# A product of the second step moved ahead of product 5 of the first, sums prepared in the head alone, and two transposes one product later

## The chip, the cores and the metric

The kernel runs on one core of one Trainium2 chip. The metric is the device time in microseconds. Three runs of the kernel before took 1656.38, 1656.97 and 1657.07 us, a median of 1656.97. The engines are named as the profile names them: PE is TensorE, DVE is VectorE, ACT is ScalarE, POOL is GpSimd and SP is SyncE. POOL and SP issue DMAs here.

## The reference

The program is a small decoder trunk on 512 tokens of 1024 features in float32, two layers deep. Each layer has a feed-forward network, a token mixer and a second feed-forward network, each with a residual and a layer norm behind it. The mixer is block-sparse attention in the first layer and multi-scale pooling in the second.

```
def swiglu(x, w_gu, w_down):
    g, u = jnp.split(x @ w_gu, 2, axis=-1)
    return (jax.nn.silu(g) * u) @ w_down

x = layer_norm(ALPHA * x + 0.5 * swiglu(x, ffn_w_gu[i, 0], ffn_w_down[i, 0]), ...)
x = layer_norm(ALPHA * x + mixer(x), ...)
x = layer_norm(ALPHA * x + 0.5 * swiglu(x, ffn_w_gu[i, 1], ffn_w_down[i, 1]), ...)
```

The inner width of the feed-forward network is 2816. The change touches neither what is computed nor the number of multiplications; it moves work.

## The kernel before, in words

**Stages.** The kernel numbers its six blocks: n=0, n=2, n=3 and n=5 are feed-forward networks (ffn), n=1 is attention and n=4 is pooling. In the profiled execution the ffn n=2 begins at about 550 us, n=3 at about 875 us, n=5 at about 1310 us. The first ffn takes another form (the flag `eight`), and the change leaves it alone.

**Products.** A float32 product is made of three matmuls: a weight tile is split into `hi` and `lo`, and lines 110, 111 and 112 add lo times x, hi times x's low part and hi times x's high part. A block of the first matrix product is not computed as eight sub-products but, in Strassen's way, as seven, numbered 1 to 7, with sums of weight blocks and sums of x blocks as operands. A step `jj` is a group of 512 inner features; the pair (i, jj) is product i of step jj. Each product has 24 matmuls of 128x512 in two halves (q = 0 and 1, each with the weights of one *unit*). `order()` at line 180 writes the order of all products by hand, since PE's queue is scheduled manually. Before the change an ffn begins (1,1), (2,1), (1,2), (5,1), (6,1), (7,1), (3,1), (4,1), (2,2), (6,2) and so on.

**Weights.** A step has two *quads*, one for each half of the contraction. A quad loads its four blocks a11, a12, a21, a22 as pieces: p11, p12, p22, and the two sums s1 = a21 + a22 and s3 = a21 + a11, which are made by a load on SP's queue (L302) and a DMA with accumulation on POOL's queue (L304). Product 6 needs p11 + s1. In steps 1 and 2 each quad makes it on VectorE in place by itself (`apart`, L158), once the accumulating DMA has landed. `prepare()` turns a unit into `hi` and `lo`: ScalarE copies hi (L105) and VectorE subtracts (L106). For the products in `BY_TRANSFER` ScalarE writes both (L336, L337) and a POOL DMA subtracts (L338). `run_ahead()` prepares as many units ahead as there is room. Only PE's order is written by hand: the recording layer schedules the instructions of the other engines and sets the order of their queues. `tc.issue_after` keeps instructions behind a named one.

**The head of an ffn.** The four token tiles t of the block before end in a layer norm: residual add (L519 in attention and pooling, L984 in an ffn), statistics (L523, L529), a square root on ScalarE, a reciprocal (L535), and the scaling of `ax` (L545). Eight PE transposes of 128x128 for each tile (L487, called T(0) to T(3) here) turn it to feature-major, and ScalarE and VectorE copy and split the result into the `x` operands. T(0) and T(1) lie in the last product of the block before. `late` holds the calls for T(2) and T(3); `head()` pops one of them after each half of (1,1). The products 1, 6 and 5 are copied out of PSUM by ScalarE (`keep`, L736); product 6 in step 1 in two halves.

**Gated rows.** A finished product pair is gated by ScalarE and VectorE (L727, L728) and then turned by four PE transposes (L761) in `to_features`. With products 5 and 4 it takes what waits in the list `waiting`.

Of the kernel before, what the change touches and what calls it, by code (L numbers as in the profile page):

```python
# [56 lines left out]
PARTS = 5  # L57
# [26 lines left out]
def trunk(ctx, tc, x_in, xt, rel_bias, ln_g, ln_b, w_gu, w_gq, w_dq, w_dh, w_v, a_in, a_out, b_in, b_group, b_scale, b_out, onehot, out):  # L84
# [34 lines left out]
            self.size = math.prod(src.shape[1:]) / 1024  # L119
            pieces.append(self)  # L120

    pieces, units, loaded, behind = [], [], [], {}

    def plain(src, lean=False):
        p = Piece(src)
        units.append((lambda: p.tile, (p,), src if lean else None))
# [51 lines left out]


    def order(eight):  # L180
        o = [(1, 1), (2, 1)] + ([(6, 1), (5, 1)] if eight else [(1, 2), (5, 1), (6, 1)])
        o += [(7, 1), (3, 1)] + [(1, 2)] * eight + [(4, 1)]
        steps = STEPS[not eight]
        for jj, following in zip(steps[1:], steps[2:] + (None,)):
            seven = [(i, jj) for i in (2, 6, 5, 7, 3, 4)]
            after = [(1, following)] if following is not None else []
            if jj == MIDDLE:
                group = [(i, FF) for i in LATER]
                o += seven[:-1] + group[:1] + seven[-1:] + group[1:] + after
            else:  # L190
                o += seven[:-1] + after + seven[-1:]
        return o + [(i, FF + 1) for i in DEEP]
# [24 lines left out]
            units.append((lambda: p.tile, (p,)))  # L217

    BY_TRANSFER = ((1, 1), (2, 1), (1, 2))

    def in_turn(quads, kinds):
        pieces[-5 * len(quads):] = [q.pieces[k] for k in kinds for q in quads]
# [18 lines left out]
    def ffn_units(l, m):  # L241
        eight = (l, m) == (0, 0)
        if eight:
            for i in FIRST:
                plain(w_gu[l, m, i])
        made = {}
        for i, jj in ORDERS[not eight]:
            lean = not eight and (i, jj) in BY_TRANSFER
            if (i, jj) == (1, 2) and not eight:
                for q in range(2):  # L250
                    plain(w_gq[l, m, 2 + q, 0], lean)
                b1 = pieces[-12:]
                pieces[-12:] = b1[0:2] + b1[4:6] + b1[2:4] + b1[10:] + b1[6:10]
                continue
            if jj not in made:
                if jj == 0:
                    made[jj] = [Quad(w_gu[l, m])]
                    pieces[-5:] = [made[jj][0].pieces[k] for k in (0, 2, 1, 3, 4)]
                elif jj == FF:
                    made[jj] = in_turn([Quad(w_dq[l, m, 0]), Quad(w_dq[l, m, 1]), narrow(Quad(w_dh[l, m]))], (0, 2, 1, 3, 4))  # L260
                elif jj == FF + 1:
                    made[jj] = in_turn([Deep(w_dq[l, m, q]) for q in (2, 3, 4)], range(5))
                else:
                    made[jj] = two_quads(w_gq[l, m], 2 * (jj - 1))
                for q in made[jj]:
                    if not eight and jj in (1, 2):
                        q.apart()
                    if i == 2:
                        q.p11.uses -= 1
            for q in made[jj]:  # L270
                q.unit(i, lean)

# [34 lines left out]
    def free():  # L307
        return SLOTS - RAW - 2 * PARTS - sum(held)
# [35 lines left out]

    def run_ahead(most=99):
        load_ahead()
        while len(parts) < min(len(units), taken[0] + most, retired[0] + PARTS + max(0, free() - 2) // 2 + early[0] + sum(i >= retired[0] for i in guests)):
            load_needed()
            prepare()
            load_ahead()  # L350
# [348 lines left out]
    def ffn(n, x, dest):  # L699
        with tc.tile_pool(name=f"ffn{n}", bufs=1) as fp:  # L700
# [47 lines left out]
                waiting.append((out, 4 * jj - 4 + 2 * half, h))  # L748
                return ins

            def to_features(i, kept_back=1):

                row = 0
                while i in (5, 4) and len(waiting) > (i == 4) * kept_back:
                    out, f, h = waiting.pop(0)
                    row += 1
                    turn[0] += row < 3
                    tp = banks(TURNED + turn[0] % 2 if row < 3 else sums_at[1], 1, f"ft{n}_{f}_{h}")[0].rearrange("p (c s) -> p c s", c=2)
                    for c in range(2):
                        for t in range(2):  # L760
                            nc.tensor.transpose(tp[:, c, t * P:(t + 1) * P], out[:, t, c * P:(c + 1) * P], ident)  # L761
                    nc.scalar.activation(features(f, 2)[:, :, h * 256:(h + 1) * 256], tp, AF.Copy)
# [177 lines left out]
            def products(i, jj, b, amid=lambda q: None, outer=3, count=2):  # L940

                if i in (1, 2, 5):
                    accs[jj, BANKS[i]] = bank_pair(((SECOND if i != 1 else sums_at[jj]) + 4 * eight) % 8)
                acc = accs[jj, BANKS[i]]

                def one(w, k0, ts, first, last):
                    wh, wl = w
                    ks = wh.shape[-1] // 512
                    for k in range(ks):
                        c = slice(k * 512, (k + 1) * 512)  # L950
                        for t in ts:
                            mm3(acc[:, t], *b(k0 + k, t), wh[:, c], wl[:, c], first and k == 0 and i in (1, 2, 5),
                                last and k == ks - 1 and i in (2, 3, 4), True)

                for q in range(min(outer, count)):
                    one(weights(), 2 * q, range(2), q == 0, q == count - 1)
                    amid(q)
                ws = [weights() for q in range(outer, count)]
                for t in range(2):
                    for q, w in enumerate(ws, outer):  # L960
                        one(w, 2 * q, (t,), q == 0, q == count - 1)
                        amid((q, t))
                return acc

            def head(i, jj):

                def amid(q):
                    if i == 1:
                        late.pop(0)()
                    if (i, q) == (1, 1):  # L970
                        while len(parts) < taken[0] + 2:
                            load_needed()
                            prepare()
                        with tc.issue_after(x.last.ins):
                            next(sums)
                return amid
# [32 lines left out]
            def down_second(i):  # L1009

                def amid(q):
                    if i == 4:
                        if q == (1, 0) and not last:
                            late.pop(0)()
                        if q != (2, 1) and q[1] == 1:
                            retire()
                    else:
                        if i == 2 and q == 2 and not last:
                            late.pop(0)()
                        if q < 2:  # L1020
                            retire()

                acc = products(i, FF + 1, operand(1, i), amid, 0 if i == 4 else 3, 3)
                half, d, sign = OUT[i]
                ts = range(2 - 2 * half, 4 - 2 * half)
                if i == 4:
                    for k, t in enumerate(ts):
                        add(t, d, acc[:, k], sign)
                        norms[t].stats(d)
                        normalized(t)  # L1030
                else:
                    add(slice(ts[0], ts[0] + 2), d, acc, sign)
                    if i in (3, 7, 2):
                        for t in ts:
                            if i != 7:
                                norms[t] = LayerNorm(n, t, 0.5)
                            norms[t].stats(d)
                    if i == 7:
                        if last:
                            params[:] = ln_params(n)  # L1040
                        for t in ts:
                            normalized(t)
                        early[0] = (2, 0, 4, 2, 0, 0)[n]
                if i == 1:
                    to_features(5)
                for _ in range({1: 2, 5: 1, 6: 1, 3: 2}.get(i, 0)):
                    next(operands[1])
                retire()

            for i, jj in ORDERS[not eight]:  # L1050
                if jj == FF:
                    down_first(i)
                    to_features(i)
                    continue
                if jj > FF:
                    down_second(i)
# [15 lines left out]
                    room(jj)  # L1072
                if jj == 0:
                    in_seven(i)
                    to_features(i)
                    retire()
                    continue
                if not eight and (i, jj) in ((1, 1), (2, 1)):
# [5 lines left out]
                if i in DONE:  # L1084
                    ins = finish(i, jj, acc)
                    if (i, jj) in RESIDUAL:
                        update_residual(ins)
                to_features(i, 2 if not eight and jj == 1 else 1)
                if not eight and (i, jj) in ((1, 1), (2, 1), (1, 2), (6, 1)):
                    if (i, jj) != (1, 1):  # L1090
                        with tc.issue_after(x.last.ins):
# [353 lines left out]
```

## Time and profile before

| what | value |
|---|---|
| median of the runs | 1656.97 us (1656.38 to 1657.07) |
| the profiled execution's own time | 1656.67 us |
| its span | 1654.9 us |
| PE busy | 1638.9 us, 99% |
| DVE busy | 1362.3 us, 82% |
| ACT busy | 953.0 us, 58% |
| POOL busy | 174.8 us, 11% |
| bytes moved by DMA | 315.62 MB, 191 GB/s over the span |

The span runs from the first to the last instruction in the trace; the time of an execution has some 1.8 us around it. In a row of the timeline stand the start in us, the duration, the engine, the line, the operation, what it writes and reads, the shape, and in square brackets how long the engine stood idle before it and what ended that. A matmul of 128x512 is shown with 0.39 us, but the next starts after 0.23 us: they are pipelined. In a row of the windows stand the stretch, its length, then for PE, weight loads, DVE, ACT and POOL the busy time and the number of instructions, and at the end the granted TensorE clock, the mean busy share of the DMA engines and GB/s. The line "DMA to landing" gives the least, the median and the greatest time from the issue of the DMAs of one line in one stretch to their landing.

### The profile page before, as it was taken

How to read it: one execution, taken by the hardware profiler on the slowest of the kernel's cores; microseconds unless marked ns; L12 is line 12 of the kernel's file. 1: busy time of each engine (PE TensorE's matmuls, PEld its weight loads, DVE VectorE, ACT ScalarE, POOL GpSimd, SP SyncE). 2: the span in 40 equal slices, each digit the busy share in tenths (PEclk: the TensorE clock that was granted, in tenths of full speed). 3: DMA queues.
4: the chain of work that ended last, by engine and by line, in shares of the span. 5: the costliest groups of instructions: out<-in, count | busy, mean ns of one | idle time of the engine just before them, and what ended most of it. 6: DMA issues, size and time to landing. Idle time of an engine off the chain costs nothing.

```text
span 1654.9 us, 21597 instructions
## 1 busy us (share of the span) xinstructions
PE 1638.9 (99%) x8051; PEld 1382.7 (84%) x8051; DVE 1362.3 (82%) x1719; ACT 953.0 (58%) x1279; POOL 174.8 (11%) x224
## 2 busy tenths in 40 slices
PE   9999999999999999999999999999999999999997
PEld 8888888898888888988888889888898878888886
DVE  7778898988575887878898878898987698779899
ACT  5556555666445665555567655556554665555562
POOL 1101101000011011101111111011000201110110
PEclk9999999999999999999999999999999999999999
DMA  9678688825157488757878887578734878866882
GB/s 300 187 224 247 151 218 227 243 71 178 52 135 197 114 242 218 201 141 212 239 214 208 251 229 186 144 214 228 225 108 125 195 201 223 245 148 176 229 205 77
DMA packets 99913, 315.62 MB, mean 191 GB/s; under 512 B 10144, under 2 KB 23496, under 8 KB 99808
## 3 DMA queue, kind: packets, MB, share of 16 engines
q1 hardware_dynamic: 71904, 214.99, 37.1%
q0 software_dynamic: 27904, 99.26, 32.7%
q8 instruction: 63, 1.03, 0.3%
q14 instruction: 42, 0.34, 0.1%
HBM read 312.09 MB, written 4.74 MB: 191 GB/s over the span
## 4 chain that ended last, share of the span: by engine, by line
PE 89%; DVE 6%; ACT 2%; issue 1%; DMA 1%; SPq 0%; DVEq 0%; ACTq 0%
PE banks L110 29%; PE banks L112 29%; PE banks L111 29%; PE banks L761 2%; DVE lo L106 2%; ACT st L495 1%; DVE x L106 1%; DVE st L429 1%; PE banks L487 1%; ACT x L105 1%; DVE st L523 1%; DVE ax L984 0%; PE banks L1194 0%; DMA raw<-in_ffn_w_gu 0%; DVE ax L542 0%
## 5 line engine op out<-in xcount | busy, mean ns | idle before, releaser
L105 ACT ACTIVATE hi<-raw 128x1024 fp32r<-128x1024 f32 (+1 forms) x478 | 500.3, 1057 | 334.2 <-DVE lo L106 121.2
L106 DVE TENSOR_TENSOR lo<-raw,hi 128x1024 fp32r<-128x1024 f32 (+1 forms) x478 | 576.8, 1218 | 130.1 <-ACT hi L105 88.3
L110 PE MATMUL banks<-lo,x 128*128 128x512 f32 x1144 | 449.3, 393 | 2.1 <-ACT kept L736 0.9
L112 PE MATMUL banks<-hi,x 128*128 128x512 f32 x1144 | 446.0, 390 | 0.0
L111 PE MATMUL banks<-hi,x 128*128 128x512 f32 x1144 | 445.4, 389 | 0.0
L110 PEld LDWEIGHTS banks<-lo,x 128*128 128x128 f32 x1144 | 214.8, 188 | 49.1 <-ACT kept L736 3.3
L112 PEld LDWEIGHTS banks<-hi,x 128*128 128x128 f32 x1144 | 214.8, 188 | 45.3
L111 PEld LDWEIGHTS banks<-hi,x 128*128 128x128 f32 x1144 | 215.0, 188 | 43.1
L110 PE MATMUL banks<-lo,h 128*128 128x512 f32 x436 | 171.4, 393 | 0.0
L112 PE MATMUL banks<-hi,h 128*128 128x512 f32 x436 | 169.8, 389 | 0.0
L111 PE MATMUL banks<-hi,h 128*128 128x512 f32 x436 | 169.7, 389 | 0.0
L110 PE MATMUL banks<-x,hi 128*128 128x256 f32 (+1 forms) x488 | 152.7, 313 | 0.5 <-ACT hi L105 0.5
L112 PE MATMUL banks<-x,lo 128*128 128x256 f32 (+1 forms) x488 | 152.0, 311 | 1.0 <-DVE lo L106 1.0
L111 PE MATMUL banks<-x,hi 128*128 128x256 f32 (+1 forms) x488 | 151.7, 311 | 0.0
L304 POOL DMA_DIRECT2D raw<-in_ffn_w_gq x80 | 71.0, 890 | 653.7 <-DMA raw<-in_ffn_w_gq 210.0
L152 DVE TENSOR_TENSOR raw<-raw,raw 128x1024 f32<-128x1024 f32 (+1 forms) x86 | 102.8, 1195 | 23.6 <-DMA raw<-in_ffn_w_gq 12.3
L110 PEld LDWEIGHTS banks<-x,hi 128*128 128x128 f32 x488 | 93.0, 191 | 6.6 <-ACT hi L105 0.9
L112 PEld LDWEIGHTS banks<-x,lo 128*128 128x128 f32 x488 | 93.0, 191 | 6.6 <-DVE lo L106 1.6
L111 PEld LDWEIGHTS banks<-x,hi 128*128 128x128 f32 x488 | 93.0, 191 | 5.3
L112 PEld LDWEIGHTS banks<-hi,h 128*128 128x128 f32 x436 | 81.8, 188 | 17.2
L111 PEld LDWEIGHTS banks<-hi,h 128*128 128x128 f32 x436 | 81.9, 188 | 16.5
L110 PEld LDWEIGHTS banks<-lo,h 128*128 128x128 f32 x436 | 81.9, 188 | 16.3
(229 smaller groups left out, 2246.0 us busy)
## 6 DMA issues: line engine op xcount, KB each, us to landing
raw<-in_ffn_w_gq SPq DMA_DIRECT2D x206, 512.0 KB, 5.0
raw<-in_ffn_w_dq SPq DMA_DIRECT2D x100, 512.0 KB, 4.8
raw<-in_ffn_w_gq POOLq DMA_DIRECT2D x80, 512.0 KB, 7.3
raw<-in_ffn_w_dq POOLq DMA_DIRECT2D x52, 512.0 KB, 7.7
ax<-in_ln_b POOLq DMA_DIRECT2D x20, 512.0 KB, 8.8
raw<-in_ffn_w_gu SPq DMA_DIRECT2D x18, 512.0 KB, 5.1
raw<-in_a_w_in SPq DMA_DIRECT2D x16, 512.0 KB, 3.8
raw<-in_ffn_w_dh SPq DMA_DIRECT2D x20, 256.0 KB, 2.8
```

What stands on the lines that cost most here:

```text
L105: nc.scalar.activation(hi, src, AF.Copy)
L106: return nc.vector.tensor_tensor(lo, src, hi.bitcast(F32), op=ALU.subtract)
L110: nc.tensor.matmul(acc, sh, ml, start=first, stop=False, skip_group_check=shared)
L111: nc.tensor.matmul(acc, sh, mh, start=False, stop=False, skip_group_check=shared)
L112: nc.tensor.matmul(acc, sl, mh, start=False, stop=last, skip_group_check=shared)
L152: nc.vector.tensor_tensor(d, d, more, op=ALU.add)
L304: queued["acc"] = nc.gpsimd.dma_start(p.tile, p.plus, accum_op=ALU.add)
L429: nc.vector.scalar_tensor_tensor(out, a, scale, b, op0=ALU.mult, op1=op)
L487: nc.tensor.transpose(tp[:, i * P:(i + 1) * P], xn[:, (4 * half + i) * P:(4 * half + i + 1) * P], ident)
L495: nc.scalar.activation(src[:, i, :], tp[:, c], AF.Identity, scale=g, bias=b)
L523: nc.vector.bn_stats(self.st[:, d * 6:d * 6 + 6], ax[:, self.t, d * 512:(d + 1) * 512])
L761: nc.tensor.transpose(tp[:, c, t * P:(t + 1) * P], out[:, t, c * P:(c + 1) * P], ident)
```

## The change

It touches the heads of the ffns n=2, n=3 and n=5 alone. Line numbers behind line 120 grow by 7 to 12: L302 becomes L309, L304 becomes L311, L487 becomes L494, L519 L526, L523 L530, L530 L537, L535 L542, L545 L552, L736 L743, L761 L768, L984 L992; L105, L106, L110 to L112 and L158 stay.

- (2,2) stands between (1,2) and (5,1), and writes to the two banks `TURNED`. Its two units are loaded as pieces of their own, so `HEAD` covers (1,2) and (2,2); the loads come in the order p11, p12, s1, then (1,2), (2,2), s3 and p22. The uses of the quads of step 2 are counted down accordingly.
- `caps` holds the number of units that stand ahead of (5,1). While an entry is at the head of the list, `run_ahead` prepares no unit from (5,1) on. The entry is taken off at the first half of (2,1), with T(3).
- T(2) follows the second half of (1,1) in place of the first, and T(3) the first half of (2,1).
- `to_features` gets the number of groups that stay in `waiting`. In step 1 it now runs with products 6, 5 and 4.

```
     def order(eight):
-        o = [(1, 1), (2, 1)] + ([(6, 1), (5, 1)] if eight else [(1, 2), (5, 1), (6, 1)])
+        o = [(1, 1), (2, 1)] + ([(6, 1), (5, 1)] if eight else [(1, 2), (2, 2), (5, 1), (6, 1)])
...
-            seven = [(i, jj) for i in (2, 6, 5, 7, 3, 4)]
+            seven = [(i, jj) for i in (2, 6, 5, 7, 3, 4)][not eight and jj == 2:]
...
+    HEAD = ((1, 2), (2, 2))
...
+            if (i, jj) == (5, 1) and not eight:
+                caps.append(len(units))
             lean = not eight and (i, jj) in BY_TRANSFER
-            if (i, jj) == (1, 2) and not eight:
+            if (i, jj) in HEAD and not eight:
                 for q in range(2):
-                    plain(w_gq[l, m, 2 + q, 0], lean)
-                b1 = pieces[-12:]
-                pieces[-12:] = b1[0:2] + b1[4:6] + b1[2:4] + b1[10:] + b1[6:10]
+                    plain(w_gq[l, m, 2 + q, i - 1], lean)
+                if i == 2:
+                    b1 = pieces[-14:]
+                    pieces[-14:] = b1[0:2] + b1[4:6] + b1[2:4] + b1[10:] + b1[6:10]
                 continue
...
+                    if i == 6:
+                        q.p11.uses -= 1
+                        q.p12.uses -= 1
...
-        while len(parts) < min(len(units), taken[0] + most, ...):
+        while len(parts) < min(len(units), (caps + [len(units)])[0], taken[0] + most, ...):
...
             def head(i, jj):
                 def amid(q):
-                    if i == 1:
+                    if (i, q) in ((1, 1), (2, 0)):
                         late.pop(0)()
-                    if (i, q) == (1, 1):
                         while len(parts) < taken[0] + 2:
                             load_needed()
                             prepare()
+                    if (i, q) == (2, 0):
+                        caps.pop(0)
                         with tc.issue_after(x.last.ins):
                             next(sums)
                 return amid
...
-                to_features(i, 2 if not eight and jj == 1 else 1)
+                opening = not eight and jj == 1
+                if i in (5, 4) or (opening and i == 6):
+                    to_features((2 if opening else 1) if i == 4 else int(opening and i == 5))
```

What the schedule makes of it is seen in the queues. In the rows below a name has its number in the program; `raw` is a loaded piece, `sm` a row of statistics, `ax` the normalized tokens.

The first place is VectorE's queue at the end of n=2, where the layer norm of the token tiles 0 and 1 leads to T(0) and T(1) of n=3. Before:

```order
L529 BN_AGGR sm2_1_7211<-st2_1_7210 128x2
L530 TENSOR_SCALAR sm2_0_7208<-sm2_0_7208 128x1
L530 TENSOR_SCALAR sm2_1_7211<-sm2_1_7211 128x1
L535 RECIPROCAL sm2_0_7208<-sm2_0_7208 128x1
L535 RECIPROCAL sm2_1_7211<-sm2_1_7211 128x1
```

With the change:

```order
L536 BN_AGGR sm2_1_7215<-st2_1_7214 128x2
L537 TENSOR_SCALAR sm2_0_7212<-sm2_0_7212 128x1
L537 TENSOR_SCALAR sm2_1_7215<-sm2_1_7215 128x1
L158 TENSOR_TENSOR raw208_7160<-raw208_7160,raw212_7253 128x1024
L542 RECIPROCAL sm2_0_7212<-sm2_0_7212 128x1
L542 RECIPROCAL sm2_1_7215<-sm2_1_7215 128x1
```

A sum for product (6,1) of n=3, the second quad's p11 plus its s1, stands between the statistics and the reciprocals; before the change all such sums stand inside the head of n=3, from about 903 us on.

The second place is VectorE's queue at the end of pooling, ahead of n=5. Before:

```order
L106 TENSOR_TENSOR lo409_10892<-raw309_10525,hi409_10891 128x1024
L519 SCALAR_TENSOR_TENSOR ax_75<-banks8_74,ax_75 128x512
L523 BN_STATS st4_0_10921<-ax_75 128x6
L519 SCALAR_TENSOR_TENSOR ax_75<-banks8_74,ax_75 128x512
L523 BN_STATS st4_0_10921<-ax_75 128x6
```

With the change:

```order
L106 TENSOR_TENSOR lo409_10900<-raw313_10533,hi409_10899 128x1024
L158 TENSOR_TENSOR raw315_10710<-raw315_10710,raw319_10842 128x1024
L526 SCALAR_TENSOR_TENSOR ax_75<-banks8_74,ax_75 128x512
L530 BN_STATS st4_0_10928<-ax_75 128x6
L526 SCALAR_TENSOR_TENSOR ax_75<-banks8_74,ax_75 128x512
L530 BN_STATS st4_0_10928<-ax_75 128x6
```

Here the same sum of n=5 stands between the last split of pooling's weights and the first residual add of the layer norm. In n=2 it stands ahead of the head too, behind the last split of the attention's probabilities.

The third place is PE's queue in the head of n=2 at T(2) (`w155` and `lo154` hold the units of (1,1), `w156` the first unit of (2,1)). Before:

```order
L111 MATMUL banks8_74<-hi154_4575,x2_1_4695 128x512
L112 MATMUL banks8_74<-hi154_4575,x2_1_4695 128x512
L487 MATMUL banks8_74<-ident_76,ax_75 128x128 x8
L110 MATMUL banks8_74<-w155_4580,x2_1_4695 128x512
L111 MATMUL banks8_74<-w155_4580,x2_1_4695 128x512
```

With the change:

```order
L111 MATMUL banks8_74<-w155_4579,x2_1_4694 128x512
L112 MATMUL banks8_74<-w155_4579,x2_1_4694 128x512
L494 MATMUL banks8_74<-ident_76,ax_75 128x128 x8
L110 MATMUL banks8_74<-w156_4583,x2_2_4705 128x512
L111 MATMUL banks8_74<-w156_4583,x2_2_4705 128x512
```

The eight transposes of token tile 2 moved behind the second half of (1,1), 12 matmuls later; those of tile 3 moved in the same way behind the first half of (2,1).

More of the change, by code (lines that the diff above doesn't have):

```diff
@@ L120, in __init__ @@
             pieces.append(self)
-    pieces, units, loaded, behind = [], [], [], {}
+    pieces, units, loaded, behind, caps = [], [], [], {}, []
     def plain(src, lean=False):
@@ L346, in run_ahead @@
         load_ahead()
-        while len(parts) < min(len(units), taken[0] + most, retired[0] + PARTS + max(0, free() - 2) // 2 + early[0] + sum(i >= retired[0] for i in guests)):
+        while len(parts) < min(len(units), (caps + [len(units)])[0], taken[0] + most, retired[0] + PARTS + max(0, free() - 2) // 2 + early[0] + sum(i >= retired[0] for i in guests)):
             load_needed()
@@ L749, in finish, with to_features @@
                 return ins
-            def to_features(i, kept_back=1):
+            def to_features(kept_back):
                 row = 0
-                while i in (5, 4) and len(waiting) > (i == 4) * kept_back:
+                while len(waiting) > kept_back:
                     out, f, h = waiting.pop(0)
@@ L942, in products @@
                 if i in (1, 2, 5):
-                    accs[jj, BANKS[i]] = bank_pair(((SECOND if i != 1 else sums_at[jj]) + 4 * eight) % 8)
+                    accs[jj, BANKS[i]] = bank_pair(((TURNED if (i, jj) == (2, 2) and not eight else SECOND if i != 1 else sums_at[jj]) + 4 * eight) % 8)
                 acc = accs[jj, BANKS[i]]
@@ L1044, in down_second @@
                 if i == 1:
-                    to_features(5)
+                    to_features(0)
                 for _ in range({1: 2, 5: 1, 6: 1, 3: 2}.get(i, 0)):
@@ L1052, in ffn @@
                     down_first(i)
-                    to_features(i)
+                    if i in (5, 4):
+                        to_features(int(i == 4))
                     continue
@@ L1074, in ffn @@
                     in_seven(i)
-                    to_features(i)
+                    if i == 5:
+                        to_features(0)
                     retire()
```

## The prediction

> **What bounds the kernel now.** I read the page's first part, then the chain that ended last, then the waits of PE.
>
> ```profile
> PE 1638.9 (99%) x8051; PEld 1382.7 (84%) x8051; DVE 1362.3 (82%) x1719; ACT 953.0 (58%) x1279; POOL 174.8 (11%) x224
> PE 89%; DVE 6%; ACT 2%; issue 1%; DMA 1%; SPq 0%; DVEq 0%; ACTq 0%
> ```
>
> TensorE is busy 99% of the span and makes 89% of the chain. So the change, which leaves the matmuls as they are, can win only the few waits of PE at the heads of the ffns it touches (n=2, n=3, n=5), and lose any new one. The timeline of PE shows the marked waits there:
>
> ```profile
> 576.09 0.50 PE L110 MATMUL banks<-lo,x 128*128 128x512 f32 x1 [0.45 <-DVE lo L106]
> 586.57 0.50 PE L110 MATMUL banks<-lo,x 128*128 128x512 f32 x1 [0.46 <-ACT kept L736]
> ...
> 888.26 1.11 PE L487 MATMUL banks<-ident,ax 128*128 128x128 f32 x8 [0.63 <-DVE ax L545]
> ...
> 1338.54 0.50 PE L110 MATMUL banks<-lo,x 128*128 128x512 f32 x1 [0.45 <-DVE lo L106]
> 1348.99 0.51 PE L110 MATMUL banks<-lo,x 128*128 128x512 f32 x1 [0.45 <-ACT kept L736]
> ```
>
> They add up to 0.45 + 0.46 + 0.63 + 0.45 + 0.45 = 2.44 us. The first instruction after each takes about 0.11 us longer than its kind (0.50 against the 0.39 of the row at 874.58 below), 0.5 us for five: some 3.0 us, or 0.18%, are there to be won.
>
> **The change, part by part.** *The moved transposes.* T(2) and T(3), eight instructions each, come 12 matmuls later. Starts of neighbouring matmuls lie 874.81 - 874.58 = 0.23 us apart (rows below), so each gets 2.7 us more for its normalized rows, above the 0.63 us of the wait at 888.26. Nothing is added. *The moved product.* (2,2) brings 24 matmuls, 5.4 us, in front of (5,1), so the split weights of (5,1) (waits of 0.45) and the copy of product 6 (0.46 and 0.45) have more cover. Price where the cover fails: the same waits again. Bounds: 3.0 us to nothing. I take 3.0, since 2.7 and 5.4 us are far above 0.63. *The transposes of gated rows.* Those of (2,2) become a group of their own, one break more in each ffn: the matmul behind a group takes 0.48 instead of 0.39 us (row at 1307.94 below), so 3 x 0.09 = 0.3 us. *Loads.* (2,2) gets its weights by two loads of its own in each ffn, six more on SP's queue. They come behind the two s1 loads in that queue, so they cannot hold these up. The rows of 1.01 to 1.07 DMA share below say that the engines are full there; a load that lands late holds up (2,2)'s split, which is a rival below.
>
> *The sum that moved ahead.* This is the term that decides. In the changed program one sum for unit (6,1), the second quad's first block plus its s1 block, stands in VectorE's queue ahead of the head: in n=3 between the two L530 and the two reciprocals of the normalization before, in n=5 ahead of its first residual add (the order rows on the change show both). The sum waits for the accumulating DMA of s1, which POOL issues. VectorE's rows follow the program's order all through the trace, so everything behind the sum waits too. What that DMA takes, from POOL's timeline and the view of that single line:
>
> ```profile
> 866.65 1.13 POOL L304 DMA_DIRECT2D raw<-in_ffn_w_gq  x1
> DMA to landing us min/median/max: 15.4/15.4/15.4
> ...
> 1290.73 0.86 POOL L304 DMA_DIRECT2D raw<-in_ffn_w_gq  x1 [2.07 <-PE banks L110]
> DMA to landing us min/median/max: 13.1/13.1/13.1
> ...
> 865.00:870.00 5.00, 5.00 (x23) 4.14 (x23) 4.97 (x6) 3.10 (x4) 2.67 (x4) 1.00 1.01 241
> 870.00:875.00 5.00, 5.00 (x24) 4.09 (x24) 3.29 (x17) 4.99 (x7) 0.84 (x1) 1.00 1.06 274
> 875.00:880.00 5.00, 5.00 (x32) 4.34 (x31) 3.71 (x6) 4.64 (x12) 0.77 (x2) 1.00 1.04 273
> 1295.00:1300.00 5.00, 5.00 (x24) 4.14 (x23) 2.17 (x4) 1.36 (x2) 0.88 (x1) 1.00 1.04 277
> ```
>
> So s1 lands at 866.65 + 15.4 = 882.05 in n=3 and at 1290.73 + 13.1 = 1303.83 in n=5. The loads and accumulations issued ahead of these two are the same in both programs, and what keeps them long, a full set of DMA engines, is there in both; so I keep the landings. The sum itself, and VectorE and PE in n=3:
>
> ```profile
> L158 DVE TENSOR_TENSOR raw<-raw,raw x24: 1215/1218/1221, 572.6 to 1375.4; 128x1024 f32<-128x1024 f32 x24
> ...
> 870.25 0.27 DVE L530 TENSOR_SCALAR sm<-sm 128x1 f32<-128x1 f32 x2
> 871.23 0.26 DVE L535 RECIPROCAL sm<-sm 128x1 f32<-128x1 f32 x2 [0.70 <-ACT sm L531]
> 872.08 1.92 DVE L545 TENSOR_SCALAR ax<-ax,sm 128x512 f32<-128x512 f32 x4
> ...
> 874.58 0.39 PE L112 MATMUL banks<-hi,h_7b 128*128 128x512 f32 x1
> 874.81 1.03 PE L487 MATMUL banks<-ident,ax 128*128 128x128 f32 x8
> ```
>
> VectorE is free at 882.05 + 1.22 = 883.27. From the first reciprocal to the end of tile 0's two halves is 872.08 + 0.96 - 871.23 = 1.81 us, so T(0) has its rows at 885.08 where PE wants them at 874.81: **PE waits 10.3 us**. Nothing covers it: PE works in order, and the matmuls behind T(0) cannot pass it. VectorE's next work then waits for PE anyway (it stood idle 1.01 us before its next add, at 875.01), so the delay is not paid twice.
>
> In n=5:
>
> ```profile
> 1293.02 1.23 DVE L106 TENSOR_TENSOR lo<-raw,hi 128x1024 fp32r<-128x1024 f32 x1 [0.18 <-ACT hi L105]
> 1296.46 0.69 DVE L519 SCALAR_TENSOR_TENSOR ax<-banks,ax 128x512 f32<-128x512 f32 x1 [2.21 <-PE banks L112]
> 1297.19 0.70 DVE L523 BATCH_NORM_STATS2 st<-ax 128x6 f32<-128x512 f32 x1
> 1299.18 0.69 DVE L519 SCALAR_TENSOR_TENSOR ax<-banks,ax 128x512 f32<-128x512 f32 x1 [1.30 <-PE banks L112]
> 1302.15 1.00 DVE L545 TENSOR_SCALAR ax<-ax,sm 128x512 f32<-128x512 f32 x2
> 1303.06 0.69 DVE L519 SCALAR_TENSOR_TENSOR ax<-banks,ax 128x512 f32<-128x512 f32 x1
> 1307.58 1.01 DVE L545 TENSOR_SCALAR ax<-ax,sm 128x512 f32<-128x512 f32 x2
> ...
> 1307.15 1.04 PE L487 MATMUL banks<-ident,ax 128*128 128x128 f32 x8
> 1307.94 0.48 PE L110 MATMUL banks<-lo,yT 128*128 128x512 f32 x1
> 1310.77 1.03 PE L487 MATMUL banks<-ident,ax 128*128 128x128 f32 x8
> ```
>
> VectorE is free at 1303.83 + 1.22 = 1305.05. Tile 0 needs 1297.89 - 1296.46 = 1.43 us for its first half and 1303.15 - 1299.18 = 3.97 us for the rest, without the waits on PE, which is far ahead by then: ready at 1310.45, wanted at 1307.15, a wait of 3.3 us. Tile 1 needs 1308.59 - 1303.06 = 5.53 us more: ready at 1315.98, wanted at 1310.77 + 3.3 = 1314.07, 1.9 us. Together **5.2 us**. Tiles 2 and 3 are transposed later than before and should take up what VectorE is then behind.
>
> In n=2 the same sum also stands ahead of the head, behind the last split of the attention's probabilities:
>
> ```profile
> 513.31 0.86 POOL L304 DMA_DIRECT2D raw<-in_ffn_w_gq  x1 [0.41 <-issue]
> DMA to landing us min/median/max: 6.6/6.6/6.6
> ...
> 521.03 0.69 DVE L106 TENSOR_TENSOR oT<-banks,oT 128x512 fp32r<-128x512 f32 x1 [5.47 <-ACT oT L105]
> ```
>
> It lands at 519.91 and the sum ends at 521.13, against 521.03 for the next work, before which VectorE is idle 5.47 us: 0.1 us, nothing for PE.
>
> **The sum.** 10.3 + 5.2 + 0.3 - 3.0 = +12.8 us on the profiled execution's own 1656.67 us (the span is 1654.9): 1669.5 us. The median of the runs, 1656.97, lies 0.3 above that execution, which I leave out. That is 0.75% slower.
>
> **Rivals.** *Not slower: s1 lands early.* The decisive point is the landing: at 874.81 - 1.81 - 1.22 = 871.78 (5.1 us after the issue) n=3 waits for nothing, and at 1307.15 - 5.40 - 1.22 = 1300.53 (9.8 us) tile 0 of n=5 doesn't either. Then the head's gain is left, 1656.67 - 2.7 = 1654.0 us. With the median of these accumulations over the whole kernel:
>
> ```profile
> raw<-in_ffn_w_gq POOLq DMA_DIRECT2D x80, 512.0 KB, 7.3
> ```
>
> n=3 would wait 2.2 us and n=5 nothing: 1656.2 us. For it speaks only this median; against it the two landings in place and the share above 1. I give it 0.13.
>
> *The clock falls in the long wait.* The rows show a granted clock of 1.00 and no idle PE longer than 0.63 us, so they cannot tell what 10.3 us of idle PE do. If matmuls then started at half rate, for nothing up to as long as the wait, 0 to 5.1 us would be lost: 1669.5 to 1674.6 us. I give a visible loss 0.17. The Trainium skill's page "TensorE: Matmul & The Clock Gate", Part 1, says that an idle window of about 3.4 us halves the clock until some 3.4 us of work have passed; by it n=3 loses 3.4 / 2 = 1.7 us more, and the time would be 1671.2 us. No run here shows it so far.
>
> *The head gets a new wait.* If (2,2)'s split weights are late by one pass of VectorE, 1.22 us, in each of the three ffns, the heads lose 3.7 us: 1673.2 us. For it: VectorE is busy for all 15 us of this stretch of n=2's head.
>
> ```profile
> 570.00:585.00 15.00, 14.55 (x65) 11.39 (x64) 15.00 (x14) 10.22 (x13) 0.86 (x1) 1.00 0.45 150
> ```
>
> Against it: 5.4 us more in front of everything behind. 0.10.
>
> **The numbers.** The forecast, the two waits with the head's gain, has 0.60, and with the clock and the head's wait "slower" has 0.87. Within the forecast the landings are the open cost: 3 us earlier each makes 1663.5 us, the head giving nothing 1672.5. The 0.13 of the early landing lies at 1654.0 to 1656.2 us, which is inside 0.2% of the 1656.97 (1653.7 to 1660.3; a measurement of this kernel hardly tells less than 0.2% from no change), so I give 0.09 to "same" and 0.04 to "faster". The range, 1661 to 1674, leaves out the early landing and the ends.
>
> **What would show it.** Right: VectorE's L158 ahead of n=3's reciprocals with an idle time of some 11 us ended by a DMA, and of some 9.6 us in n=5; PE's L494 for T(0) waiting some 10 us for ax in n=3, 3 us and 2 us for T(0) and T(1) in n=5; the waits quoted first gone or below 0.3 us; a granted clock below 1.00 behind n=3's wait would show the second rival. Wrong: PE without a wait of more than 1 us ahead of the heads; or the sum running without idle time in front of it.

## The result, and the profile after

The changed kernel takes 1671.73 us in the median of five runs (1671.32 to 1673.54), against 1656.38 us (1655.42 to 1657.07) for the kernel before on the same chip. The ratio is 1.0094 with a 95% interval of 1.0083 to 1.0105: some 15 us slower. The forecast was 1669.5 us, in a range of 1661 to 1674.

The page's first part and chain of the changed kernel, and from its list of waits the one that grew:

```profile
PE 1641.7 (98%) x8051; PEld 1386.2 (83%) x8051; DVE 1362.2 (82%) x1719; ACT 951.4 (57%) x1279; POOL 175.2 (10%) x224
PE 91%; DVE 5%; DMA 2%; ACT 1%; issue 1%; SPq 0%; DVEq 0%; ACTq 0%; POOLq 0%
...
PE banks L494 <- DVE ax L552: 14.4, 3, 10.0
```

The columns of the last row are the total, the count and the longest wait in us. DVE's total is as before (1362.2 against 1362.3): nothing was added to it, its work was only put in another order. PE's busy time is 2.8 us longer for the same instructions, and DMAs are now 2% of the chain, against 1% before.

VectorE's and PE's timeline ahead of n=3 in the changed kernel, and POOL's landing of the s1 accumulation:

```profile
869.07 0.27 DVE L537 TENSOR_SCALAR sm<-sm 128x1 f32<-128x1 f32 x2
880.70 1.22 DVE L158 TENSOR_TENSOR raw<-raw,raw 128x1024 f32<-128x1024 f32 x1 [11.36 <-DMA raw<-in_ffn_w_gq]
881.84 0.21 DVE L542 RECIPROCAL sm<-sm 128x1 f32<-128x1 f32 x2
...
872.86 0.39 PE L112 MATMUL banks<-hi,h_7b 128*128 128x512 f32 x1
883.28 1.97 PE L494 MATMUL banks<-ident,ax 128*128 128x128 f32 x8 [10.03 <-DVE ax L552]
...
L311 POOL DMA_DIRECT2D raw<-in_ffn_w_gq x1: 1476/1476/1476, 865.1 to 865.1; - x1
DMA to landing us min/median/max: 15.6/15.6/15.6
```

The sum stands where the order of the queue put it, between the statistics and the reciprocals. VectorE is idle for 11.36 us in front of it until the DMA issued at 865.1 lands 15.6 us later, and PE's transposes T(0) wait 10.03 us. The same ahead of n=5:

```profile
1314.59 1.23 DVE L158 TENSOR_TENSOR raw<-raw,raw 128x1024 f32<-128x1024 f32 x1 [11.14 <-DMA raw<-in_ffn_w_gq]
1315.73 0.68 DVE L526 SCALAR_TENSOR_TENSOR ax<-banks,ax 128x512 f32<-128x512 f32 x1
1320.00 1.00 DVE L552 TENSOR_SCALAR ax<-ax,sm 128x512 f32<-128x512 f32 x2
...
1299.39 0.87 POOL L311 DMA_DIRECT2D raw<-in_ffn_w_gq  x1 [1.52 <-PE banks L112]
DMA to landing us min/median/max: 15.2/15.2/15.2
...
1320.60 1.60 PE L494 MATMUL banks<-ident,ax 128*128 128x128 f32 x8 [4.09 <-DVE ax L552]
1325.91 1.03 PE L494 MATMUL banks<-ident,ax 128*128 128x128 f32 x8
```

Behind both waits PE is slow for a while. The windows show it in the granted clock, the number ahead of the DMA share; 1.00 is full speed:

```profile
883.00:888.00 5.00, 4.72 (x16) 4.12 (x17) 4.60 (x8) 3.57 (x10) 0.00 (x0) 0.55 1.07 229
888.00:893.00 5.00, 5.00 (x27) 4.20 (x27) 2.91 (x7) 4.61 (x9) 1.76 (x2) 1.00 0.20 25
1320.60:1325.00 4.40, 4.40 (x17) 3.74 (x18) 3.89 (x11) 0.88 (x4) 0.00 (x0) 0.61 0.01 4
```

From 883.28 to 888 the clock is lacking 0.45 of 4.7 us, 2.1 us; from 1320.6 to 1325 it is lacking 0.39 of 4.4 us, 1.7 us. So the loss is made of 10.0 and 4.1 us of waiting and 3.8 us of slow matmuls, 17.9 us, less what the heads gained, some 2.6 us by the kernel below with the sum between the transposes and the head: 15.3 us.

The heads did become shorter. Of the five waits quoted before, those on lo and on ax are gone, and the two on the copy of product 6 have shrunk from 0.46 and 0.45 to 0.2 us each. In n=2:

```profile
590.05 0.50 PE L110 MATMUL banks<-lo,x 128*128 128x512 f32 x1 [0.21 <-ACT kept L743]
```

### The profile page after: what moved, and what is told of

It is laid out like the page before. It is cut to its first block, busy times and chain, and to the rows that moved or that the text cites. A ratio compares the mean times of both kernels' runs of the same rounds, so it can differ in the third digit from the quotient of the medians.

```text
span 1669.6 us, 21617 instructions
## 1 busy us (share of the span) xinstructions
PE 1641.7 (98%) x8051; PEld 1386.2 (83%) x8051; DVE 1362.2 (82%) x1719; ACT 951.4 (57%) x1279; POOL 175.2 (10%) x224
## 4 chain that ended last, share of the span: by engine, by line
PE 91%; DVE 5%; DMA 2%; ACT 1%; issue 1%; SPq 0%; DVEq 0%; ACTq 0%; POOLq 0%
PE banks L110 29%; PE banks L112 29%; PE banks L111 29%; PE banks L768 2%; DMA raw<-in_ffn_w_gq 2%; PE banks L494 1%; DVE lo L106 1%; DVE st L530 1%; DVE x L106 0%; PE banks L1206 0%; DVE ax L992 0%; DMA raw<-in_ffn_w_gu 0%; ACT hi L105 0%; DVE ax L549 0%; DVE ax L540 0%
## 5 line engine op out<-in xcount | busy, mean ns | idle before, releaser
L105 ACT ACTIVATE hi<-raw 128x1024 fp32r<-128x1024 f32 (+1 forms) x478 | 499.7, 1056 | 332.4 <-DVE lo L106 121.8
L106 DVE TENSOR_TENSOR lo<-raw,hi 128x1024 fp32r<-128x1024 f32 (+1 forms) x478 | 577.1, 1218 | 133.1 <-ACT hi L105 91.0
L110 PE MATMUL banks<-lo,x 128*128 128x512 f32 x1144 | 449.1, 393 | 0.5 <-ACT kept L743 0.4
L112 PE MATMUL banks<-hi,x 128*128 128x512 f32 x1144 | 445.9, 390 | 0.0
L110 PEld LDWEIGHTS banks<-lo,x 128*128 128x128 f32 x1144 | 214.8, 188 | 46.3 <-issue 0.9
L112 PEld LDWEIGHTS banks<-hi,x 128*128 128x128 f32 x1144 | 214.7, 188 | 45.2
L110 PE MATMUL banks<-lo,h 128*128 128x512 f32 x436 | 172.0, 394 | 0.0
L112 PE MATMUL banks<-hi,h 128*128 128x512 f32 x436 | 170.2, 390 | 0.0
L110 PE MATMUL banks<-x,hi 128*128 128x256 f32 (+1 forms) x488 | 152.7, 313 | 0.0
L112 PE MATMUL banks<-x,lo 128*128 128x256 f32 (+1 forms) x488 | 151.8, 311 | 0.7 <-DVE lo L106 0.7
L311 POOL DMA_DIRECT2D raw<-in_ffn_w_gq x80 | 71.2, 900 | 643.1 <-DMA raw<-in_ffn_w_gq 194.4
L112 PEld LDWEIGHTS banks<-x,lo 128*128 128x128 f32 x488 | 93.1, 191 | 5.9 <-DVE lo L106 0.9
L110 PEld LDWEIGHTS banks<-x,hi 128*128 128x128 f32 x488 | 93.2, 191 | 5.6 <-DVE oT L106 0.2
L112 PEld LDWEIGHTS banks<-hi,h 128*128 128x128 f32 x436 | 82.1, 188 | 17.4
L110 PEld LDWEIGHTS banks<-lo,h 128*128 128x128 f32 x436 | 82.2, 188 | 16.4
```

Source lines behind the costliest of these rows:

```text
L105: nc.scalar.activation(hi, src, AF.Copy)
L106: return nc.vector.tensor_tensor(lo, src, hi.bitcast(F32), op=ALU.subtract)
L110: nc.tensor.matmul(acc, sh, ml, start=first, stop=False, skip_group_check=shared)
L112: nc.tensor.matmul(acc, sl, mh, start=False, stop=last, skip_group_check=shared)
L311: queued["acc"] = nc.gpsimd.dma_start(p.tile, p.plus, accum_op=ALU.add)
```

## The experiments

### The sum alone

The kernel before, with the hold taken from the preparation behind (1,2). The schedule then puts the sum for (6,1) of the second quad at the same three places as in the changed kernel; nothing else of the change is in it. (A sum of x that stands under the same hold loses it too.)

```
-                        with tc.issue_after(x.last.ins):
+                        with tc.issue_after(x.last.ins) if (i, jj) != (1, 2) else ExitStack():
```

> The kernel before with one thing of the change alone: the sum for (6,1) of the second quad is left to the schedule without a hold, so it stands ahead of the head in VectorE's queue in the same three places as in the changed kernel. Theory (the sum that waits for its accumulating DMA is the whole loss): the changed kernel's PE waits come back, about 10 us at T(0) of n=3 and about 4 us in n=5, and with them two stretches at half clock (about 2.1 and 1.7 us lost): the time is that of before + 18 us, some 1674 us, 3 us above the changed kernel, since the head's gain is missing. Rival (the moved product and its loads make the loss, the sum only fills a hole): within 2 us of before, 1655 to 1659 us.

Measured: 1674.9 us (1673.74 to 1676.39) against 1656.75, ratio 1.0113 (1.0099 to 1.0127), +18.2 us. Its timeline:

```profile
881.37 1.23 DVE L158 TENSOR_TENSOR raw<-raw,raw 128x1024 f32<-128x1024 f32 x1 [11.56 <-DMA raw<-in_ffn_w_gq]
883.95 0.47 PE L487 MATMUL banks<-ident,ax 128*128 128x128 f32 x1 [9.51 <-DVE ax L545]
...
1317.42 1.23 DVE L158 TENSOR_TENSOR raw<-raw,raw 128x1024 f32<-128x1024 f32 x1 [11.57 <-DMA raw<-in_ffn_w_gq]
1323.44 0.47 PE L487 MATMUL banks<-ident,ax 128*128 128x128 f32 x1 [4.53 <-DVE ax L545]
```

Both waits come back without the moved product, its loads or the moved transposes, and so does the slow clock behind them. The sum ahead of its landing makes the whole loss: 18.2 us here, 17.9 us in the changed kernel, whose heads then win some of it back.

### The sum held to the end of the head

The changed kernel, with the preparation behind (2,2) held as it is behind (1,2) and (2,1).

```
                 else:
-                    retire(2)
+                    with tc.issue_after(x.last.ins) if not eight and (i, jj) == (2, 2) else ExitStack():
+                        retire(2)
```

> The changed kernel, in which the preparation behind (2,2) is held behind the last split of x, as it is behind (1,2) and (2,1); all sums then stand inside the heads. Theory: the two waits and the half-rate stretches go, the head's gain of 2.5 to 3.0 us stays: 1653.5 to 1654.5 us where before takes 1656.7, ratio 0.9980 to 0.9988. Rival (the change slows the heads themselves, by the loads or the new product's weights): 1657 us or more. Second rival (the sum was one late landing among several; another piece of work stands in VectorE's queue in its place): a PE wait of 5 us or more for ax at T(0) of n=3.

Measured: 1663.35 us (1662.22 to 1664.13), ratio 1.0041 (1.0027 to 1.0055), +6.6 us. The waits for ax are gone, and still the kernel is slower than before. The time is that of the first rival, but the reason is neither the loads nor the new product's weights: a new wait stands in each head, of 2.35 to 2.55 us, at the split of the very sum that was held, that of the second half of (6,1). Here is n=2, PE and then VectorE:

```profile
590.29 0.50 PE L110 MATMUL banks<-lo,x 128*128 128x512 f32 x1 [2.55 <-DVE lo L106]
...
585.01 0.68 DVE L735 SCALAR_TENSOR_TENSOR gated<-kept,gated 128x512 f32<-128x512 f32 x1
585.62 3.49 DVE L158 TENSOR_TENSOR raw<-raw,raw 128x1024 f32<-128x1024 f32 x3
589.02 2.35 DVE L106 TENSOR_TENSOR lo<-raw,hi 128x1024 fp32r<-128x1024 f32 x2
```

and the same stretch of the changed kernel:

```profile
583.95 0.69 DVE L735 SCALAR_TENSOR_TENSOR gated<-kept,gated 128x512 f32<-128x512 f32 x1
584.55 1.22 DVE L106 TENSOR_TENSOR lo<-raw,hi 128x1024 fp32r<-128x1024 f32 x1
586.00 1.22 DVE L106 TENSOR_TENSOR lo<-raw,hi 128x1024 fp32r<-128x1024 f32 x1 [0.23 <-ACT hi L105]
587.14 1.22 DVE L158 TENSOR_TENSOR raw<-raw,raw 128x1024 f32<-128x1024 f32 x1
588.28 1.22 DVE L106 TENSOR_TENSOR lo<-raw,hi 128x1024 fp32r<-128x1024 f32 x1
```

With the sum held, three sums stand in a row ahead of the split that PE wants next. With the sum done before the head, that split comes first. So the early sum, which costs 18 us where it waits, is also what makes the heads short. The 6.6 us add up: 7.5 us for the three waits and 1.7 us for a slow clock behind the one in n=3 (last section), less the 2.6 us. My step "I take 3.0" had costed the heads as if the sum's place did not matter to them.

### The transposes alone

The kernel before, with T(2) and T(3) half a product later.

```
-                    if i == 1:
+                    if (i, q) in ((1, 1), (2, 0)):
                         late.pop(0)()
```

(A second preparation of two units behind the first half of (2,1), and the call of `next(sums)` there, come with them, as in the change; so not the transposes alone are moved.)

> The kernel before with T(2) and T(3) one half product later and nothing else. Theory: only the wait of 0.63 us at T(2) of n=3 goes: 0.6 to 0.8 us faster than before, ratio 0.9995 to 0.9997; the waits on lo at product 5 and on the copy at product 7 stay. Rival (the moved transposes hold back the sums of x, and products 5 and 6 wait longer): 1 us or more slower than before.

Measured: 1666.56 us (1666.49 to 1669.77), ratio 1.0066 (1.0054 to 1.0079), +9.8 us: the rival, with ten times the least price that I had named. The wait at T(2) of n=3 is gone, but PE waits on lo in eight places, 10.3 us in all. Two of them, and what held VectorE ahead of the second:

```profile
PE banks L110 <- DVE lo L106: 10.3, 8, 2.6
...
579.58 0.50 PE L110 MATMUL banks<-lo,x 128*128 128x512 f32 x1 [1.09 <-DVE lo L106]
600.30 0.50 PE L110 MATMUL banks<-lo,x 128*128 128x512 f32 x1 [2.51 <-DVE lo L106]
...
597.89 1.22 DVE L158 TENSOR_TENSOR raw<-raw,raw 128x1024 f32<-128x1024 f32 x1 [2.57 <-DMA raw<-in_ffn_w_gq]
```

At 597.89 it is again a sum that waits for a landing in front of a split. What makes the other waits was not followed.

### The product alone

As the kernel with the sum held to the end of the head, but T(2) and T(3) at their places of before (`if i == 1: late.pop(0)()`).

> As the second kernel of this call, but T(2) and T(3) at their places of before: the moved product without the moved transposes. Theory: the waits on lo and on the copy in n=2 and n=5 go (some 2 us), the wait at T(2) of n=3 stays: 1.5 to 2.3 us faster than before, ratio 0.9986 to 0.9991. Rival (the gain needs both parts): not faster than before by more than 0.5 us.

Measured: 1657.27 us (1656.44 to 1659.24), ratio 1.0005 (0.9996 to 1.0014): no difference that can be told. The rival held. The waits on lo at product 5 are gone, a wait on the lo of the second half of (6,1) stands in n=2 and n=5:

```profile
587.21 0.50 PE L110 MATMUL banks<-lo,x 128*128 128x512 f32 x1 [1.17 <-DVE lo L106]
```

### The sum between the transposes and the head

The changed kernel, with the preparation behind (2,2) held behind the last split that was there when the ffn began, which is that of token tile 1.

```
+            opened = None if eight else x.last
             for i, jj in ORDERS[not eight]:
...
                 else:
-                    retire(2)
+                    with tc.issue_after(opened.ins) if not eight and (i, jj) == (2, 2) else ExitStack():
+                        retire(2)
```

> The changed kernel, in which the preparation behind (2,2) is held behind the last split of token tile 1 only: in all three ffns the same single sum then stands between the transposes of T(1) and the head, in n=3 some 14 us later in VectorE's queue than in the changed kernel and after the landing of its DMA, in n=5 some 25 us later. Theory (two things set the time: where the sum waits for its landing, and that it is out of the way of the splits in the head): no wait for ax above 1 us, no half-rate stretch, and the heads as short as in the changed kernel: 1653.5 to 1655.0 us where before takes 1656.7, ratio 0.9980 to 0.9990. Rival (the splits of product 6 are late whenever the sum isn't done before the head begins to compete): waits on lo of 1 to 2.6 us in the heads as with the sum held to the end, 1658 us or more.

Measured: 1653.45 us in the median of eleven runs (1652.25 to 1655.47) against 1656.08 us, ratio 0.9984 (0.9975 to 0.9992): 2.6 us faster than before, and so some 18 us faster than the changed kernel. The sum in n=3 and n=5, and T(0) of both:

```profile
883.13 1.22 DVE L158 TENSOR_TENSOR raw<-raw,raw 128x1024 f32<-128x1024 f32 x1
1316.16 1.21 DVE L158 TENSOR_TENSOR raw<-raw,raw 128x1024 f32<-128x1024 f32 x1
...
873.44 1.03 PE L494 MATMUL banks<-ident,ax 128*128 128x128 f32 x8
1304.41 1.03 PE L494 MATMUL banks<-ident,ax 128*128 128x128 f32 x8
...
PE banks L110 <- ACT kept L743: 0.4, 2, 0.2
```

None of these rows of L158 and L494 has an idle time in brackets: the sum finds its piece landed, and the transposes find their rows. This kernel beats both others. What separates it from the changed kernel is the place of one preparation, with one sum, in each of three ffns, and the 18 us are the 17.9 us of the two waits and the two slow stretches.

### Which parts the gain needs

Three more kernels put that sum between T(1) and the head, and leave one or both of the other parts out. The first is the kernel before with nothing but the sum moved there:

```
-                        with tc.issue_after(x.last.ins):
+                        with tc.issue_after((opened if (i, jj) == (1, 2) else x.last).ins):
```

> The kernel before, with nothing but the same sum placed between T(1) and the head. Theory (the moved product and the moved transposes give the gain, the sum only must not stand in their way): the waits for lo and for the copy remain for the most part, 0 to 1.2 us faster than before, ratio 0.9993 to 1.0000. Rival (the early sum is the whole gain, and the moved product is not needed): 2.5 us or more faster than before.

Measured: 1658.05 us (1657.09 to 1661.22), ratio 1.0011 (1.0003 to 1.0020), slightly slower than before, outside both. The 1.2 us more ahead of T(2) in n=3 let PE wait there longer than the 0.63 us of before, and the waits on lo (L110) add up to 3.0 us where they were 0.9. The profiled execution took 1659.39 us, 1.3 above the median. The wait at T(2) in it:

```profile
890.14 0.33 PE L487 MATMUL banks<-ident,ax 128*128 128x128 f32 x1 [1.55 <-DVE ax L545]
```

The second has the product and the sum there, with T(2) and T(3) as before (`if i == 1: late.pop(0)()`).

> The moved product and the sum placed between T(1) and the head, T(2) and T(3) at their places of before. Theory (all three parts are needed, since the early sum takes 1.2 us of VectorE just ahead of T(2)): the wait for ax at T(2) of n=3 grows from 0.63 to about 1.6 us, as it did with the kernel before and the early sum; the other heads lose less than 1 us each: 1654.5 to 1656 us where before takes 1656.4. Rival (the moved transposes add nothing to the product and the sum): 1653.0 to 1654.0 us, as with all three.

Measured: 1656.49 us (1655.12 to 1660.39), ratio 1.0002 (0.9993 to 1.0011). That is no gain that can be told, and 0.5 us above the range expected. The profiled execution took 1660.39 us and is the longest of the eleven, so its waits need not be those of the median: 1.86 us at T(2) of n=3, near the 1.6 expected, and 2.81 us for `kept` further on in n=3, which I had not named. Ahead of the second, VectorE's sums wait 4.85 us for a landing. The rows stand below, with the clock. The third has the transposes and the sum there, with (2,2) at its place of before: the first diff of this section on top of the moved transposes.

> The moved transposes and the sum placed between T(1) and the head, product (2,2) at its place of before. Theory (without 24 matmuls more in front of product 5 the splits of products 5 and 6 are late again, since the sums of x come later): waits on lo of 0.5 us and more in each head, 1657 to 1662 us where before takes 1656.4. Rival (it is the held sum alone that made the moved transposes slow): 1653.0 to 1655.0 us.

Measured: 1658.8 us (1658.37 to 1660.2), ratio 1.0017 (1.0008 to 1.0026), as the theory had it, with waits on lo in all three heads; the longest is 1.67 us in n=3. Together, as ratios to the kernel before:

| sum | T(2), T(3) as before | T(2), T(3) later |
|---|---|---|
| in the head, (2,2) as before | 1 (the kernel before) | 1.0066 |
| in the head, (2,2) ahead | 1.0005 | 1.0041 |
| between T(1) and the head, (2,2) as before | 1.0011 | 1.0017 |
| between T(1) and the head, (2,2) ahead | 1.0002 | 0.9984 |

No part gains anything alone, and no two parts do. With all three the heads gain 2.6 us. The cells differ by more than their headings say. With (2,2) ahead come its loads and the turning of its gated rows; the second preparation and the later `next(sums)` come with it and with the later T(2) and T(3) alike. What each of these is worth alone was not measured. That VectorE's order in the head is what the parts share is shown for the three sums in a row; for the other cells the waits are shown, and which of VectorE's instructions stands in the way was not followed in each.

### How long a wait makes the clock fall

The kernel with the sum between T(1) and the head, with work added on VectorE for token tile 0 ahead of n=3, which multiplies it by one and leaves its values as they are:

```
+            if (self.n, t) == (2, 0):
+                for _ in range(2):
+                    ins = nc.vector.tensor_scalar(r, r, 1.0, None, op0=ALU.mult)
             return None if last else ins
```

> The first kernel of this call with work added on VectorE: token tile 0 of the layer norm before n=3 is multiplied by one twice more, so that T(0) comes late and PE waits some 1.2 us once. Theory (the clock falls only when PE is idle for most of a stretch of 3.4 us): the granted clock stays 1.00 and the kernel takes 1 to 1.5 us more than the first of this call. Rival (any wait above 1 us halves the clock): a half-rate stretch and 2.5 us or more.

Measured: 1653.82 us (1652.97 to 1655.29), ratio 0.9985 (0.9976 to 0.9994). PE did not wait at T(0): a multiplication took 0.6 us from one start to the next and not the 1.0 I had put in, so VectorE still had room. This run says nothing on the clock, but it shows that the two multiplications, 1.2 us, can be hidden ahead of T(0). With three multiplications:

> As the kernel before it, with three multiplications: PE waits some 3.4 us once at T(0) of n=3. Theory (a free-running stretch of 3.4 us must be nearly empty): the clock falls in some executions and not in others, by where the wait lies; the time is 3.4 us above the first of this call without the fall and 5.1 us with it. Rival (the clock falls only when the wait is longer than 4 us): never, always 3.4 us.

Measured: 1656.59 us (1655.18 to 1660.84), ratio 1.0004 (0.9995 to 1.0013), 3.1 us above the kernel without them. In the profiled execution:

```profile
872.43 0.39 PE L112 MATMUL banks<-hi,h_7b 128*128 128x512 f32 x1
874.91 1.26 PE L494 MATMUL banks<-ident,ax 128*128 128x128 f32 x8 [2.09 <-DVE ax L555]
...
872.28:875.69 3.41, 1.32 (x10) 0.90 (x9) 3.41 (x6) 2.73 (x3) 1.93 (x3) 1.00 1.03 270
875.69:879.11 3.42, 3.42 (x11) 2.74 (x10) 0.36 (x1) 2.02 (x5) 0.72 (x1) 0.50 1.07 280
```

The wait was 2.09 us, not the 3.4 expected, and it was enough, so the rival (never below 4 us) falls. The theory's "nearly empty" falls too: the clock went down at 875.69, when PE had been at work again for 0.8 us, and in the 3.41 us ahead of that PE had been busy for 1.32 us. Whether the clock fell in the other nine executions no trace shows.

## Why the prediction was right, and where its sizes were off

**What bounds the kernel, and where the loss comes from.** Right in place and cause. The terms against their measurements:

| step | forecast | measured |
|---|---|---|
| n=3, wait for ax at T(0) | 10.3 us | 10.03 us |
| n=5, waits for ax at T(0) and T(1) | 3.3 + 1.9 = 5.2 us | 4.09 us at T(0), none at T(1); the rest of the 14.4 us is a wait of 0.24 us at 342.81, ahead of the attention |
| n=2 | 0.1 us on VectorE, nothing for PE | no wait for ax there |
| gain of the heads | 3.0 - 0.3 = 2.7 us | 2.6 us, as the kernel without the waits shows |
| slow clock behind the waits | a rival, 0 to 5.1 us | 2.1 + 1.7 = 3.8 us |
| time | 1669.5 us | 1671.73 us |

**n=3.** The landing kept its length, as assumed: 15.6 us from the issue against 15.4 before. That the wait came out so near is in part luck: from the first reciprocal to T(0) it took 883.28 - 881.84 = 1.44 us and not the 1.81 summed, for the reason given under n=5, and the longer landing made up half of it.

**n=5.** The step that was mis-sized, in three places that partly cancel, which is luck too. The landing took 15.2 us here, not the 13.1 of before. From the next row's start at 1315.73 to T(0) at 1320.60 it took 4.9 us, not 5.40: T(0) starts when the first of the two scaled halves is there (the L552 row at 1320.00, of which a half is 0.5 us), and I had waited for both. And the second wait, 1.9 us, vanished: PE ran at half clock between T(0) and T(1), which then lie 5.31 us apart and not 3.62. What was to be waiting appeared as slow work.

**The heads.** "3.0, since 2.7 and 5.4 us are far above 0.63" came out right in size and was wrong in its reason, so the size is luck. More matmuls in front of a product were no cover where VectorE's order put other work first: the product and the transposes together lose 6.6 us without the early sum. The third rival, "the head gets a new wait", is near what happens in that case, but the split that is late is that of (6,1) and not (2,2)'s, by some 2.5 us and not 1.22. The forecast held because the same early sum that made the loss also made the gain. The 0.3 us for the third group of gated rows was not measured apart.

**The clock.** This rival, with a chance of 0.17, came true on top of the forecast. I took nothing for it because no row of before had a PE wait above 0.63 us; it is the largest term that the sum lacked, 3.8 us. The Trainium skill's page "TensorE: Matmul & The Clock Gate", Part 1, gives a half rate for about 3.4 us of work behind an idle window of about that length, by estimate 1.7 us. The trace agrees: n=5 lost 1.7 us, and n=3 lost 2.1. With 1.7 us for each of the two waits the sum would have been 1672.9 us. Where the Trainium skill's page asks for an idle window of the full 3.4 us, the runs differ: the last section shows the clock falling behind waits of 2 us, and the measurement decides.

**Not slower** fell: neither landing came early.

## What to carry to other kernels

When an edit moves instructions between queues, read where each one lands in every in-order queue and what it waits for there: here a 1.2 us sum put ahead of the landing of its DMA, in two ffns, cost 14 us of waiting and 3.8 us of slow matmuls on TensorE, far from the code that was edited. The same instruction put behind the landing, in a stretch where VectorE had room, turned the loss into a gain. Parts that share a busy engine need not add up; here all three together were faster, and any two of them were not.

## What the runs showed of the hardware

A short wait of TensorE can have a price behind it. PE waits of 1.86 us and, further on, 2.81 us (product and sum ahead), 2.09 us (three multiplications), 2.35 us (n=3 of the sum held to the end) and 4.09 us (the changed kernel) were each followed by a stretch at a granted clock of 0.50, 3.41 us long, which costs some 1.7 us where all of it falls on work. Behind the 4.53 us of the kernel with the sum alone the stretch was twice as long, and 5.93 us of it fell on work: some 3.0 us. Waits of 1.67 us (transposes and sum), 2.51 and 2.57 us (transposes alone) and 2.55 us (n=2 and n=5 of the sum held) were followed by none. So the length of the wait alone does not decide. In the kernel with the product and the sum ahead but not the transposes:

```profile
887.09 0.33 PE L494 MATMUL banks<-ident,ax 128*128 128x128 f32 x1 [1.86 <-DVE ax L552]
...
930.45 2.54 DVE L158 TENSOR_TENSOR raw<-raw,raw 128x1024 f32<-128x1024 f32 x2 [4.85 <-DMA raw<-in_ffn_w_gq]
935.31 0.50 PE L110 MATMUL banks<-lo,x 128*128 128x512 f32 x1 [2.81 <-DVE kept L753]
...
885.01:888.42 3.41, 1.55 (x11) 1.25 (x11) 3.26 (x14) 1.68 (x4) 0.87 (x1) 1.00 1.07 264
888.42:891.83 3.41, 3.41 (x10) 2.62 (x9) 1.27 (x3) 2.89 (x8) 0.78 (x1) 0.50 1.06 213
```

Here the clock fell at 888.42, 1.3 us after PE had gone on. What decides, by these traces, is where the wait lies. Within each trace the clock changes on a grid: any two changes ahead of the end are 3.41 us or a whole multiple of it apart, as the 10.24 us from 877.30 to 887.54 in the changed kernel. Where the grid lies differs from trace to trace. The kernel with the sum held to the end shows what it does, in n=3 and in n=5; the number behind the length is PE's busy time:

```profile
919.79:923.20 3.41, 1.48 (x6) 1.24 (x7) 3.41 (x4) 1.46 (x2) 0.88 (x1) 1.00 0.81 243
923.20:926.61 3.41, 3.41 (x12) 2.73 (x10) 2.17 (x3) 1.87 (x3) 0.87 (x1) 0.50 0.92 210
...
1353.28:1356.69 3.41, 1.68 (x8) 1.04 (x6) 3.41 (x4) 2.58 (x4) 0.86 (x1) 1.00 0.48 167
1356.69:1360.10 3.41, 2.59 (x11) 2.15 (x12) 3.41 (x4) 0.61 (x2) 0.87 (x1) 1.00 0.80 268
```

In n=3 most of the wait of 2.35 us lies in one stretch of the grid; PE is busy there for 1.48 of 3.41 us, and the next stretch is at half clock. In n=5 the wait is longer, 2.55 us, but lies across two stretches, and the clock stays. Over the twelve traces every fall stands behind a stretch in which PE was idle for 1.86 us or more, and no stretch with 1.83 us or less has one behind it. Inside the kernels the clock rose again only behind a stretch in which PE was busy throughout: with the sum alone, 0.89 us of idle time in n=5 kept it low for a second stretch. The ends of matmuls are modelled in the profile, so the second decimal of the limit is not firm.

An accumulating DMA of 512 KB took 15.2 and 15.6 us to land where the DMA engines had a busy share of 1.00 to 1.07, against a median of 7.3 us over the kernel before. The share alone does not tell how long one takes: the one ahead of n=2 took 6.6 us in the kernel before at a share of 0.95 (513 to 520 us).
